# A RWKV-7 chunk scan with joint PSUM banks, and a Mamba-2 stage in another order: one encoder layer on one core

## The chip, the cores and the metric

The kernel runs as one program on one core of a Trainium2 chip. The metric is device time in microseconds, the median of several executions. For the kernel before, three executions gave 2464.68, 2473.31 and 2473.44 us, median 2473.31. Engine names are those of the profile: PE is TensorE's matmuls, PEld its weight loads, DVE VectorE, ACT ScalarE, POOL GpSimd, SP SyncE.

## The reference

One layer of a bidirectional encoder, 1024 tokens by 1024 channels, all in float32. One wide input projection feeds three branches (Mamba-2, RWKV-7, HGRN2) and three gates; each branch scans in both directions and adds the two; the branches are projected, gated and summed, projected again, and a SwiGLU feed-forward follows. The two parts that matter here:

```python
# Mamba-2, one direction, chunks of 128 tokens, 16 heads x 64, 2 groups, state 128
a_cum = cumsum(dt * a)                      # per head, within the chunk
y_diag = (C B^T * exp(a_cum[q] - a_cum[s]), s <= q) @ (x * dt)
chunk_state = B^T @ (x * dt * exp(a_cum[-1] - a_cum))
S = exp(a_cum[-1]) * S + chunk_state        # from chunk to chunk
y_off = (C @ S_prev) * exp(a_cum)
y = y_forward + y_backward + x * d_skip;  y = rmsnorm(y * silu(z))
# RWKV-7, per head 64 x 64 state, both directions
S_t = S_{t-1} diag(w_t) + (S_{t-1} (-kk_t)) (kk_t a_t)^T + v_t k_t^T;  y_t = S_t r_t
```

## The kernel before, in words

**Fillers.** The input projection is float32 in three passes: each step is three matmuls of 128x128 weights by 128x512 (lines 329 to 331, `mm<-x,wh` and `mm<-x,wl`), 16 steps to a job, into one of three PSUM banks of the tag `mm`. A job loads a weight tile `wr`, ScalarE casts it to `wh` (line 220), and VectorE or GpSimd makes the rest `wl` (line 222). The steps are dealt out between the work of the branches, so that PE has something to do in their waits: `J.fill(n)` issues n steps, `J.share(w)` issues the part `w / J.weight` of what is left. The tables `FILL` hold these numbers. The order on each engine is set by a scheduler, except where a block is under `manual_schedule`: there the named engine keeps the order in which the code is written. Finished halves are copied by ScalarE to `st` (line 271) and stored.

**RWKV chunk scan** (stage `r2`, lines 734 to 890, 444 to 637 us of the span). 16 chunks of 64 tokens, two directions d, 8 heads as 4 pairs. For each chunk and direction: `G`, products of B/K with A/R, 8 matmuls into two banks of the tag `g` (two banks in all, shared with the transposes `Bps`), masked into SBUF by VectorE in four operations (lines 805 and 807); `R` = G x SV, copied by ScalarE; `U` = T x R, which VectorE and ScalarE write negated into `UV`; `S` += B^T x UV, scaled by VectorE into the next chunk's `SV`; `Y` = UV x G + SV x A/R in two groups of 8. G of the next chunk is made while R, U and S of this one wait. Each direction has banks and tiles of its own, so most evacuations are 128x256. One filler step follows U, one follows Y. The scheduler orders PE.

**Mamba-2 stage** (`ssd`, 1128 to 1481 us). For each of two groups of 8 heads: convolutions (lines 1279 to 1289) of B, C and four tiles of x; C B^T (`CB`) and transposes of B and x to token-major `Bt`, `xt`; then a loop of 8 steps i, in which direction 0 handles chunk i and direction 1 chunk 7 - i. `pairs(c)` makes the 128 x 8 x 128 matrix E of chunk c: two DMAs fetch rows of `cumd` broadcast to all partitions, GpSimd subtracts the column values (line 1357), VectorE merges the two directions with a predicated copy (line 1360), ScalarE takes the exponential (1361), VectorE multiplies by CB (1362). It is called two steps ahead, rows and all. In each step and direction: `yo` = C x S, one matmul 128x512 (1378), `yt` = yo x e^cum on VectorE (1380), Y += yt on GpSimd (1381), `xw` = xt x weights on VectorE (1384), `st` = B x xw on PE (1386), S x decay on GpSimd (1390), S += st on VectorE (1391). Then 8 `yd` products with E as weights (128 columns) and 64 columns of xt moving (1397), added to Y by VectorE (1399). The skip term starts Y: GpSimd writes Y = xt x gd (1371). GpSimd's order in the loop is as written. After a group's loop, the end phase: silu of z (1408), 32 transposes of Y (1417), the product with z (1418), the store to `ysc`, squares (1425) and their sums (1426). Tiles `E`, the convolutions' and z's share five buffers (`EB = 5`).

Of the kernel before, what the change touches and what calls it, by code (L numbers as in the profile page):

```python
# [18 lines left out]
P = 128  # L19
# [19 lines left out]
    "ss": (4, 36, 12, 18, 6, 3, 8, 5, 22, 13, 8),  # L39
# [344 lines left out]
def rwkv(g):  # L384
# [349 lines left out]
    with ExitStack() as es:  # L734
# [16 lines left out]
        S = []  # L751
        for d in range(2):
            t = rp.tile([P, 4, 64], F32, tag=f"S{d}", name=f"S{d}", bufs=1)
            nc.gpsimd.memset(t, 0.0)
            S.append(t)
        NS = 16

        def load_early(c, d):
            if c >= NS:
                return None  # L760
            AR = rp.tile([P, 4, 2, 64], F32, tag=f"AR{d}", name="ARc", bufs=3)
            BK = rp.tile([P, 4, 2, 64], F32, tag=f"BK{d}", name="BKc", bufs=3)
            TT = rp.tile([P, 4, 64], F32, tag=f"TT{d}", name="TTc", bufs=3)
            nc.sync.dma_start(BK, BKs[d][:, c].rearrange("p q (s t) -> p q s t", s=2))
            nc.sync.dma_start(AR, ARs[d][:, c].rearrange("p q (s t) -> p q s t", s=2))
            nc.sync.dma_start(TT, TTs[:, d, c])
            return AR, BK, TT

        def loads(c, d, early):
            AR, BK, TT = early  # L770
            UV = rp.tile([P, 2, 4, 64], F32, tag=f"UV{d}", name="UVc")
            SV = rp.tile([P, 2, 4, 64], F32, tag=f"SV{d}", name="SVc")
            G = rp.tile([P, 2, 4, 2, 64], F32, tag=f"G{d}", name="Gc")
            cc = c if d == 0 else NS - 1 - c
            vs = Vs[cc // 2, (cc % 2) * 64:(cc % 2) * 64 + 64]
            for e in range(2):
                er = slice(e * 64, e * 64 + 64)
                nc.gpsimd.tensor_scalar(G[er, e, :, 0, :], AR[er, :, 0, :], 1.0, None, MUL)
            for t in (SV, UV):
                nc.sync.dma_start(t[64:128, 0], vs[:, 0])  # L780
                nc.sync.dma_start(t[0:64, 1], vs[:, 1])
            if c == 0:
                nc.gpsimd.memset(SV[0:64, 0], 0.0)
                nc.gpsimd.memset(SV[64:128, 1], 0.0)
            return AR, BK, UV, SV, TT, G

        def prep_b(c, d, ld):
            BK = ld[1]
            Bt = rp.tile([P, 4, P], F32, tag=f"Bt{d}", name="Btc")
            ps = pp.tile([P, 4, P], F32, tag="g", name="Bps", bufs=2)  # L790
            for p in range(4):
                nc.tensor.transpose(ps[:, p], BK[:, p].rearrange("p s t -> p (s t)"), g.ident)
            nc.scalar.copy(Bt, ps)
            return Bt

        def prep_g(c, d, ld):
            AR, BK, UV, SV, TT, G = ld
            pss = [pp.tile([P, 4, 2, 64], F32, tag="g", name="Gps", bufs=2) for e in range(2)]
            for p in range(4):
                for e in range(2):  # L800
                    er = slice(e * 64, e * 64 + 64)
                    nc.tensor.matmul(pss[e][:, p], BK[er, p], AR[er, p], start=True, stop=True)  # L802
# [7 lines left out]
        HD = [(h % 2, h // 2, slice(h % 2 * 64, h % 2 * 64 + 64)) for h in range(8)]  # L810

        def c_R(c, d, ld):
            AR, BK, UV, SV, TT, G = ld
            R = rp.tile([P, 4, 64], F32, tag=f"R{d}", name="Rc")
            psR = pp.tile([P, 4, 64], F32, tag="c", name="Rps", bufs=2)
            for e, p, er in HD:
                nc.tensor.matmul(psR[er, p], G[:, e, p, 0, :], SV[:, e, p, :], start=True, stop=True)
            nc.scalar.copy(R, psR)
            return R

        def c_U(c, d, ld, R):
            AR, BK, UV, SV, TT, G = ld
            psU = pp.tile([P, 4, 64], F32, tag="c", name="Ups", bufs=2)
            for e, p, er in HD:
                nc.tensor.matmul(psU[er, p], TT[er, p], R[er, p], start=True, stop=True)
            nc.vector.tensor_scalar(UV[0:64, 0], psU[0:64], -1.0, None, MUL)
            nc.scalar.mul(UV[64:128, 1], psU[64:128], -1.0)

        def c_S(c, d, ld, Bt, nxt):
            AR, BK, UV, SV, TT, G = ld  # L830
            psS = pp.tile([P, 4, 64], F32, tag="c", name="Sps", bufs=2)
            for e, p, er in HD:
                nc.tensor.matmul(psS[er, p], Bt[:, p, er], UV[:, e, p, :], start=True, stop=True)
            pc = PC[:, d, c].unsqueeze(2).broadcast_to([P, 4, 64])
            nc.vector.tensor_add(S[d], S[d], psS)
            SVn = nxt[3]
            nc.vector.tensor_mul(SVn[0:64, 0], S[d][0:64], pc[0:64])
            nc.vector.tensor_mul(SVn[64:128, 1], S[d][64:128], pc[64:128])
            nc.gpsimd.tensor_mul(S[d], S[d], pc)

        def c_Y(c, d, ld):
            AR, BK, UV, SV, TT, G = ld
            pool, tag, n = (pp, "y", 1) if d == 0 else (g.mmps, "mm", 3)
# [1280 lines left out]
```

## Time and profile before

| | us |
|---|---|
| median of 3 executions | 2473.31 |
| the profiled execution | 2473.65 |
| its span, first to last instruction | 2471.9 |
| outside the span | 1.75 |
| PE busy in the span | 2309.0 (93%) |
| granted TensorE clock, mean | 0.968 |
| RWKV chunk scan, 444 to 637 | 193 |
| Mamba-2 stage, 1128 to 1481 | 353 |

A page of the profile gives busy times by engine; views of the trace give groups of instructions by line, waits, and a timeline. A matmul's length in the timeline overlaps the next one's, so its cost is read from start to start. "Idle before" names what an engine waited for last. A float32 matmul shows as two records.

### The profile page before, as it was taken

The numbers are of one execution on the slowest core, as the hardware profiler recorded it, in microseconds if no ns is written. First come the engines' busy times: TensorE is split into PE (matmuls) and PEld (weight loads), VectorE is DVE, ScalarE is ACT, GpSimd is POOL, SyncE is SP. The second block draws the span as 40 slices with busy tenths as digits, with TensorE's granted clock in tenths as the row PEclk, the third lists the DMA queues.
The fourth block names the chain that finished last, engine by engine and source line by source line (L and its number), as shares of the span: only waits on it lengthen the run. The fifth ranks groups of instructions, "written<-read, shape, count | busy, mean of one in ns | idle before, by whom it ended". The sixth has DMA issues, their size and how long they took to land.

```text
span 2471.9 us, 37794 instructions
## 1 busy us (share of the span) xinstructions
PE 2309.0 (93%) x14785; PEld 1865.5 (75%) x14785; DVE 1633.4 (66%) x2130; ACT 989.0 (40%) x1460; POOL 1070.9 (43%) x863
## 2 busy tenths in 40 slices
PE   8998999999989889999899899999999999999985
PEld 6777778888867777778668667788788888877664
DVE  5678863456567867746666676643675455569999
ACT  6554532222454654436224236322433333344333
POOL 4433422444134543320661671421464444447885
PEclk9999999899999999999899999999899999999998
DMA  5456685654342232225635647632132222253311
GB/s 148 122 140 137 161 211 123 201 169 147 118 148 90 82 111 78 73 73 172 149 114 170 149 111 248 211 111 95 60 95 85 86 79 84 86 179 111 97 66 68
DMA packets 381215, 306.27 MB, mean 124 GB/s; under 512 B 111273, under 2 KB 323149, under 8 KB 381037
## 3 DMA queue, kind: packets, MB, share of 16 engines
q1 hardware_dynamic: 260909, 225.71, 30.8%
q10 hardware_dynamic: 119936, 77.61, 10.8%
q8 instruction: 117, 1.92, 0.3%
q0 software_dynamic: 192, 0.52, 0.1%
q14 instruction: 61, 0.50, 0.1%
HBM read 209.68 MB, written 94.11 MB: 123 GB/s over the span
## 4 chain that ended last, share of the span: by engine, by line
PE 60%; DVE 23%; POOL 5%; issue 5%; DMA 4%; ACT 3%; ACTq 0%; SPq 0%; DVEq 0%; POOLq 0%
PE mm L329 6%; PE mm L330 6%; PE mm L331 6%; PE ps L1576 6%; PE ps L1577 6%; PE ps L1578 6%; DVE acc L1915 3%; DVE ab L1793 2%; PE Gps L802 2%; PE mm L232 2%; PE mm L230 2%; PE mm L231 2%; DMA E<-cumd 2%; POOL E L1357 2%; DVE rb L1793 1%
## 5 line engine op out<-in xcount | busy, mean ns | idle before, releaser
L329 PE MATMUL mm<-x,wh 128*128 128x512 f32 (+1 forms) x1232 | 499.4, 405 | 0.5 <-ACT wh L220 0.5
L330 PE MATMUL mm<-x,wh 128*128 128x512 f32 (+1 forms) x1232 | 495.7, 402 | 0.0
L331 PE MATMUL mm<-x,wl 128*128 128x512 f32 (+1 forms) x1232 | 494.2, 401 | 0.2
L329 PEld LDWEIGHTS mm<-x,wh 128*128 128x128 f32 (+1 forms) x1232 | 234.1, 190 | 61.7 <-issue 10.6
L331 PEld LDWEIGHTS mm<-x,wl 128*128 128x128 f32 (+1 forms) x1232 | 233.9, 190 | 56.4 <-issue 6.0
L330 PEld LDWEIGHTS mm<-x,wh 128*128 128x128 f32 (+1 forms) x1232 | 234.4, 190 | 55.6 <-issue 6.8
L1578 PE MATMUL ps<-xb,rb 128*128 128x512 f32 x432 | 168.1, 389 | 0.0
L1576 PE MATMUL ps<-xb,rb 128*128 128x512 f32 x432 | 168.0, 389 | 0.0
L1577 PE MATMUL ps<-xb,rb 128*128 128x512 f32 x432 | 168.0, 389 | 0.0
L220 ACT CAST wh<-wr 128x1024 fp32r<-128x1024 f32 (+2 forms) x103 | 100.2, 973 | 118.8 <-PE mm L330 96.7
L1576 PE MATMUL ps<-rb,ab 128*128 128x512 f32 x308 | 125.8, 408 | 20.1 <-DVE acc L1915 19.1
L222 POOL TENSOR_TENSOR wl<-wr,wh 128x1024 fp32r<-128x1024 f32 x30 | 78.2, 2607 | 146.6 <-ACT wh L220 137.4
L222 DVE TENSOR_TENSOR wl<-wr,wh 128x1024 fp32r<-128x1024 f32 (+2 forms) x73 | 97.2, 1332 | 62.2 <-ACT wh L220 62.2
L1577 PE MATMUL ps<-rb,ab 128*128 128x512 f32 x308 | 122.4, 397 | 2.4 <-POOL rb L1793 2.4
L1578 PE MATMUL ps<-rb,ab 128*128 128x512 f32 x308 | 121.5, 397 | 1.5 <-DVE ab L1793 1.5
L1740 ACT CAST rb<-fs 128x512 fp32r<-128x512 f32 x85 | 52.5, 622 | 167.3 <-PE ps L1578 115.7
L271 ACT COPY st<-mm 128x512 f32<-128x512 f32 x130 | 75.6, 581 | 97.5 <-PE mm L331 77.8
L805 DVE TENSOR_TENSOR Gc<-Gps,mk 128x256 f32<-128x256 f32 x64 | 27.0, 422 | 112.0 <-PE Gps L802 59.1
L1915 DVE TENSOR_TENSOR acc<-acc,ps 128x512 f32<-128x512 f32 x148 | 94.1, 675 | 0.2 <-PE ps L1578 0.2
L1576 PEld LDWEIGHTS ps<-xb,rb 128*128 128x128 f32 x432 | 81.1, 188 | 16.9
L1578 PEld LDWEIGHTS ps<-xb,rb 128*128 128x128 f32 x432 | 81.1, 188 | 16.8
L1577 PEld LDWEIGHTS ps<-xb,rb 128*128 128x128 f32 x432 | 81.1, 188 | 16.7
(504 smaller groups left out, 5548.9 us busy)
## 6 DMA issues: line engine op xcount, KB each, us to landing
wr<-in_w_in_dram ACTq DMA_DIRECT2D x74, 512.0 KB
fr<-in_ffn_w_in_dram SPq DMA_DIRECT2D x44, 512.0 KB
E<-cumd SPq DMA_DIRECT2D x32, 512.0 KB
pg<-st ACTq DMA_DIRECT2D x48, 256.0 KB
gt<-pg SPq DMA_DIRECT2D x24, 512.0 KB
ad<-a SPq DMA_DIRECT2D x22, 512.0 KB
dr<-in_ffn_w_down_dram SPq DMA_DIRECT2D x22, 512.0 KB
ar<-ad SPq DMA_DIRECT2D x22, 512.0 KB
```

What stands on the lines that cost most here:

```text
L220: nc.scalar.copy(hi[:, :kt, :n], raw[:, :kt, :n])
L222: g.lo_eng.tensor_sub(lo[:, :kt, :n], raw[:, :kt, :n], f32(hi[:, :kt, :n]))
L271: g.nc.scalar.copy(st[:n], ps)
L329: g.nc.tensor.matmul(ps[:n], w[0][:, k, :n], xh, start=(k == 0), stop=False)
L330: g.nc.tensor.matmul(ps[:n], w[0][:, k, :n], xl, start=False, stop=False)
L331: g.nc.tensor.matmul(ps[:n], w[1][:, k, :n], xh, start=False, stop=(k == KT - 1))
L1576: nc.tensor.matmul(ps, ah, bh, start=(i == 0), stop=False)
L1577: nc.tensor.matmul(ps, ah, bl, start=False, stop=False)
L1578: nc.tensor.matmul(ps, al, bh, start=False, stop=(i == n - 1))
L1740: nc.scalar.copy(blk[:, 0], src[j])
L1793: eng.tensor_sub(blk[:, 1], s, f32(blk[:, 0]))
L1915: nc.vector.tensor_add(m[j], m[j], ps)
```

## The change

Two stages are rewritten; the rest keeps its text and gets new line numbers.

Chunk scan: both directions share tiles (`S`, `SV`, `UV`, `R`) and one PSUM bank for each of R, U, S and Y, so one evacuation of 128x512 stands for two of 128x256. Direction 1's G products go to the `mm` banks. The code of a chunk stands under `manual_schedule(engines={PE})`, so PE keeps the order as written: R, G of direction 0, U, filler, G of direction 1, S, B, Y, filler.

Mamba-2: the output is made channel-major. `yd` takes 64 columns of xt as weights and E (128 columns) as the moving side; `yo` takes four 128-column slices of the state as weights and C as the moving side; the transposes of the end phase disappear. e^cum is now the tile `X`, exponentials of the fetched rows on ScalarE, multiplied by yo on VectorE. Adding the column values is ScalarE's for direction 0 (eight 128x128 operations with a bias) and GpSimd's for direction 1. Direction 1's seven states are made in a prepass into `Sb`, between `pairs(0)` and `pairs(1)`; the loop carries only direction 0's state `Sa`, whose decay product is VectorE's. The skip term is put on E's diagonal by a second predicated copy (`id8`). silu(z) is made before the prepass and staged in DRAM (`zd`); each step loads its part, multiplies, stores to `ysc`, and adds the squares in small GpSimd operations. `rows(i + 2)` is called at the top of step i, `pairs(i + 2)` at its end. The table `FILL["ss"]` changes: 551 parts before, 573 after; between the first chunk's rows and the loop's end stand 187 of them for each group (7 x 5 + 8 x 10 + 8 x 9).

```diff
-    "ss": (4, 36, 12, 18, 6, 3, 8, 5, 22, 13, 8),
+    "ss": (4, 30, 12, 5, 10, 9, 22, 8, 5),
...
-        def prep_g(c, d, ld):
-            AR, BK, UV, SV, TT, G = ld
-            pss = [pp.tile([P, 4, 2, 64], F32, tag="g", name="Gps", bufs=2) for e in range(2)]
+        def prep_g(d, ld):
+            G = ld.G[d]
+            pool, tag, n = (pp, "g", 2) if d == 0 else (g.mmps, "mm", 3)
+            pss = [pool.tile([P, 512], F32, tag=tag, name="Gps", bufs=n).rearrange("p (q s t) -> p q s t", q=4, s=2)
+                   for e in range(2)]
...
+        def c_R(ld):
+            R = rp.tile([P, 2, 4, 64], F32, tag="R", name="Rc")
+            psR = bank("c", "Rps", 2)
+            for d, e, p, er in HD:
+                nc.tensor.matmul(psR[er, d, p], ld.G[d][:, e, p, 0, :], ld.SV[:, d, e, p, :], start=True, stop=True)
+            nc.scalar.copy(R, psR)
+            return R
...
+        order = ExitStack()
+        order.enter_context(tc.manual_schedule(engines={PE}))
         for c in range(NS):
...
+            R = c_R(ld)
             J.fill(F[0] + (F[6] if c < 2 else 0))
             if c + 1 < NS:
-                prep_g(c + 1, 0, nx[0])
-            for d in range(2):
-                c_U(c, d, ld[d], R[d])
+                prep_g(0, nx)
+            c_U(ld, R)
             J.fill(F[1])
             if c + 1 < NS:
-                prep_g(c + 1, 1, nx[1])
-                for d in range(2):
-                    c_S(c, d, ld[d], bt[d], nx[d])
+                prep_g(1, nx)
+                c_S(c, ld, bt, nx)
                 J.fill(F[2])
-                bt = [prep_b(c + 1, d, nx[d]) for d in range(2)]
-            for d in range(2):
-                c_Y(c, d, ld[d])
+                bt = [prep_b(d, nx) for d in range(2)]
+            c_Y(c, ld)
             J.fill(F[3])
...
+                for q in range(grp * 4, grp * 4 + 4):
+                    zs = sp.tile([P, L + 4], F32, tag="E", name="zs", bufs=EB)[:, :L]
+                    nc.sync.dma_start(zs, J.get(g.pz, q))
+                    nc.scalar.activation(zs, zs, AF.Silu)
+                    nc.sync.dma_start(zd[q], zs)
...
+                def pairs(c, Es):
+                    Xs = []
+                    for d in range(2):
+                        e, h0 = Es[d], d * 16 + grp * 8
+                        X = yp.tile([P, 4, P], F32, tag=f"X{d}", name="X", bufs=2)
+                        if c != (0, NT - 1)[d]:
+                            for b in range(2):
+                                hr = slice(b * 64, b * 64 + 64)
+                                nc.scalar.activation(X[hr], e[hr, b::2], AF.Exp)
+                        if d == 0:
+                            for h in range(8):
+                                nc.scalar.activation(e[:, h], e[:, h], AF.Identity, bias=cums[:, c, h0 + h:h0 + h + 1])
+                        else:
+                            nc.gpsimd.tensor_tensor(e, e, cums[:, c, h0:h0 + 8].unsqueeze(2).broadcast_to([P, 8, P]),
+                                                    ADD)
...
                     nc.vector.tensor_mul(e, e, CB[:, c:c + 1, :].broadcast_to([P, 8, P]))
+                    nc.vector.copy_predicated(e, id8.unsqueeze(1).broadcast_to([P, 8, P]),
+                                              gd[:, c].unsqueeze(2).broadcast_to([P, 8, P]))
...
+                def state(d, c, old, new):
+                    xw = yp.tile([P, 512], F32, tag="xw", name="xw", bufs=2)
+                    nc.vector.tensor_tensor(h3(xw), h3(xt[:, c]), per_head(wst, c, d), MUL)
+                    ps = pp.tile([P, 512], F32, tag="b", name="st", bufs=2)
+                    nc.tensor.matmul(ps, Bt[:, c], xw, start=True, stop=True)
+                    if old is None:
+                        nc.vector.tensor_copy(new, ps)
+                    else:
+                        (nc.vector if d == 0 else nc.gpsimd).tensor_tensor(h3(new), h3(old), per_head(dec, c, d), MUL)
+                        nc.vector.tensor_add(new, new, ps)
...
+                nxt = [pairs(0, rows(0))]
+                ahead = rows(1)
+                for c in range(NT - 1, 0, -1):
+                    state(1, c, Sb[:, c] if c < NT - 1 else None, Sb[:, c - 1])
+                    J.share(F[3])
+                nxt.append(pairs(1, ahead))
                 for i in range(NT):
...
+                    e, X = nxt.pop(0)
+                    if i + 2 < NT:
+                        ahead = rows(i + 2)
+                    part = []
+                    for d, S in ((1, Sb[:, i] if i < NT - 1 else None), (0, Sa if i else None)):
...
+                        for q in range(4):
+                            nc.tensor.matmul(ps[:, q], S[:, q * P:(q + 1) * P], CT[:, ts], start=True, stop=True)
+                        nc.vector.tensor_mul(X[d], X[d], ps)
+                        part.append(X[d])
+                    if i < NT - 1:
+                        state(0, i, Sa if i else None, Sa)
+                    J.share(F[4])
...
+                        nc.tensor.matmul(ps[h % 2 * 64:h % 2 * 64 + 64, h // 2], xt[:, i, h * 64:h * 64 + 64], e[:, h],
                                          start=True, stop=True)
...
+                        nc.gpsimd.tensor_add(y, y, part[1])
+                    nc.vector.tensor_add(y, y, ps)
+                    nc.vector.tensor_mul(z, z, y)
+                    nc.sync.dma_start(ysc[grp * 4:grp * 4 + 4, :, ts].rearrange("q p t -> p q t"), z)
+                    nc.scalar.activation(y, z, AF.Square)
...
+                    if i + 2 < NT:
+                        nxt.append(pairs(i + 2, ahead))
                     J.share(F[5])
```

How the order on the engines moves. PE in one chunk of the scan, before (R, G, U, S, B and Y are the `ps` tiles; each row is one line's matmuls in succession):

```order
L817 MATMUL Rps<-SVc,Gc 64x64 x16
L802 MATMUL Gps<-ARc,BKc 128x128 x8
L825 MATMUL Ups<-Rc,TTc 64x64 x16
L802 MATMUL Gps<-ARc,BKc 128x128 x8
L848 MATMUL Yps<-Gc,UVc 64x64 x2
L833 MATMUL Sps<-UVc,Btc 64x64 x16
L792 MATMUL Bps<-ident,BKc 128x128 x4
L848 MATMUL Yps<-Gc,UVc 64x64 x4
L792 MATMUL Bps<-ident,BKc 128x128 x4
L848 MATMUL Yps<-Gc,UVc 64x64 x3
L850 MATMUL Yps<-ARc,SVc 64x64 x8
```

And in the changed kernel, where `mm` are filler matmuls:

```order
L823 MATMUL Rps<-SV,Gc 64x64 x16
L806 MATMUL Gps<-ARc,BKc 128x128 x8
L830 MATMUL Ups<-Rc,TTc 64x64 x16
L329 MATMUL mm<-x_208,wh 128x512
L330 MATMUL mm<-x_209,wh 128x512
L331 MATMUL mm<-x_208,wl 128x512
L806 MATMUL Gps<-ARc,BKc 128x128 x8
L837 MATMUL Sps<-UV,Btc 64x64 x16
L793 MATMUL Bps<-ident,BKc 128x128 x8
L849 MATMUL Yps<-Gc,UV 64x64 x16
L852 MATMUL Yps<-ARc,SV 64x64 x16
```

The second G group now has a filler step ahead of it, and S, B and Y stand in whole groups.

VectorE in the Mamba-2 loop, before (`m` is the mask of the predicated copy, the two `S` the two directions' states):

```order
L1360 COPY_PREDICATED E<-m_10446,E 128x1024
L1384 TENSOR_TENSOR xw<-xt,wst 128x512
L1391 TENSOR_TENSOR S_10889<-S_10889,st 128x512
L1362 TENSOR_TENSOR E<-E,CB 128x1024
L1380 TENSOR_TENSOR yt<-yo,ecum 128x512
L1399 TENSOR_TENSOR Y<-Y,yd 128x512
L1391 TENSOR_TENSOR S_10888<-S_10888,st 128x512
```

And after, about one step of the loop:

```order
L1380 COPY_PREDICATED E<-m_10222,E 128x1024
L1436 TENSOR_TENSOR X<-X,yd 128x512
L1424 TENSOR_TENSOR X<-X,yo 128x512
L1399 TENSOR_TENSOR Sa<-Sa,dec 128x512
L1437 TENSOR_TENSOR z<-z,X 128x512
L1393 TENSOR_TENSOR xw<-xt,wst 128x512
L1400 TENSOR_TENSOR Sa<-Sa,st 128x512
L1382 TENSOR_TENSOR E<-E,CB 128x1024
L1383 COPY_PREDICATED E<-id_10223,gd 128x1024
```

The decay, the z product and the id8 copy are new on VectorE; the predicated copy of a later chunk stands ahead of the addition of `yd`.

GpSimd in the same loop, before:

```order
L1390 TENSOR_TENSOR S_10888<-S_10888,dec 128x512
L1357 TENSOR_TENSOR E<-E,cums 128x1024 x2
L1381 TENSOR_TENSOR Y<-Y,yt 128x512
L1390 TENSOR_TENSOR S_10889<-S_10889,dec 128x512
L1381 TENSOR_TENSOR Y<-Y,yt 128x512
```

And after:

```order
L1376 TENSOR_TENSOR E<-E,cums 128x1024
L1435 TENSOR_TENSOR X<-X 128x512
L1442 TENSOR_TENSOR X<-X 128x256
L1444 TENSOR_TENSOR ss<-X 128x128
```

One E product instead of two, one addition instead of two, no state products in the loop, and the two small sums.

More of the change, by code (lines that the diff above doesn't have):

```diff
@@ L808, in prep_g @@
                                         mk[d][e][kr, 0].unsqueeze(1).broadcast_to([64, 4, 64]), MUL)
[L810 to L817, printed above, removed]
+        HD = [(d, h % 2, h // 2, slice(h % 2 * 64, h % 2 * 64 + 64)) for d in range(2) for h in range(8)]
@@ L1343, in h3, with rows @@
                     return t.rearrange("p (h v) -> p h v", v=64)
-                S = [yp.tile([P, 512], F32, tag=f"S{d}", name=f"S{d}") for d in range(2)]
-                J.share(F[3])
-                def pairs(c):
+                def rows(c):
                     Es = []
```

248 lines of the change are left out of this document (105 added, 143 removed).

## The prediction

> **What bounds the kernel now.** The page first: TensorE (PE) is busy for 93% of the span, so time can only be won where PE's work shrinks or where it waits. Then the two stages that the change touches, by windows (length; busy us of PE, PEld, DVE, ACT, POOL; granted clock, DMA share, GB/s):
>
> ```profile
> PE 2309.0 (93%) x14785; PEld 1865.5 (75%) x14785; DVE 1633.4 (66%) x2130; ACT 989.0 (40%) x1460; POOL 1070.9 (43%) x863
> ```
>
> ```profile
> 444.00:637.00 193.00, 191.65 (x3240) 163.07 (x3239) 110.99 (x266) 50.91 (x116) 74.29 (x92) 0.96 0.52 159
> ```
>
> ```profile
> 1128.00:1186.00 58.00, 58.00 (x310) 48.12 (x309) 37.74 (x39) 36.42 (x50) 2.52 (x8) 1.00 0.50 133
> 1186.00:1300.00 114.00, 100.70 (x414) 71.89 (x414) 77.64 (x70) 26.36 (x30) 80.69 (x49) 0.91 0.49 130
> 1300.00:1375.00 75.00, 75.00 (x377) 63.27 (x376) 47.87 (x44) 35.82 (x45) 11.39 (x17) 1.00 0.56 170
> 1375.00:1481.00 106.00, 96.03 (x411) 68.88 (x409) 75.92 (x70) 27.06 (x32) 79.32 (x49) 0.95 0.54 128
> ```
>
> 444 to 637 is the RWKV chunk scan, where PE seems never to wait. The other four rows are the Mamba-2 stage, 353 us: convolutions of group 0, its chunk loop, convolutions of group 1, its loop. The convolution parts, 58 + 75 = 133 us, are full of PE work. In the loops, 114 and 106 us, PE is idle for 13 and 10 us and runs at clocks of 0.91 and 0.95, and POOL has more to do than DVE.
>
> Whether the scan is full of work is seen in the timeline of one chunk (start, length, operation; then VectorE at the same time):
>
> ```profile
> 466.31 1.15 PE L817 MATMUL Rps<-SVc,Gc 128*64 128x64 f32 x32
> ...
> 582.23 1.15 PE L817 MATMUL Rps<-SVc,Gc 128*64 128x64 f32 x32
> 583.31 1.16 PE L802 MATMUL Gps<-ARc,BKc 64*128 64x128 f32 x16
> 584.40 1.15 PE L825 MATMUL Ups<-Rc,TTc 64*64 64x64 f32 x32
> 585.48 1.94 PE L802 MATMUL Gps<-ARc,BKc 64*128 64x128 f32 x16
> 587.35 0.45 PE L848 MATMUL Yps<-Gc,UVc 128*64 128x64 f32 x4
> ...
> 593.86 1.15 PE L817 MATMUL Rps<-SVc,Gc 128*64 128x64 f32 x32
> ...
> 619.77 1.15 PE L817 MATMUL Rps<-SVc,Gc 128*64 128x64 f32 x32
> ```
>
> ```profile
> 584.51 0.42 DVE L805 TENSOR_TENSOR Gc<-Gps,mk 128x256 f32<-128x256 f32 x1 [1.74 <-PE Gps L802]
> ...
> 585.75 0.41 DVE L807 TENSOR_TENSOR Gc<-Gps,mk 64x256 f32<-64x256 f32 x1
> ```
>
> Both G groups are the same work, but from start to start the first takes 584.40 - 583.31 = 1.09 us, the second 587.35 - 585.48 = 1.87: it waits for the two banks that VectorE empties until 586.16. So 0.78 us of each chunk is a wait that is counted as busy. A chunk takes (619.77 - 466.31) / 13 = 11.80 us, the one shown 593.86 - 582.23 = 11.63.
>
> **Chunk scan: -13 us.** PE keeps the same matmuls. The second G group now takes its banks from the fillers' three, so its wait goes: 11.63 - 0.78 = 10.85; I take 10.8, 1.0 less in each of those 13 chunks. The joint evacuations (128x512 for two of 128x256) lie beside PE and count nothing. What covers each operand in the new order: the copy of R lies under the first G group (1.09), UV (after four evacuations of 0.42) under the fillers and the second G group, the next SV under B, Y and the fillers. With 0.78 in each chunk and no more it is -10; if new waits eat it, zero (a rival); PE gets no new work, so a loss could only come from those waits.
>
> **Mamba-2: PE's work.** The filler line by total and in the two loops, PE's pace on fillers, and three prices (start to start):
>
> ```profile
> L330 PE MATMUL mm<-x,wh 128*128 128x512 f32 x314 | 129.7, 413 | 0.0
> ```
>
> ```profile
> 1186.00:1300.00 114.00, 33.78 (x76) 14.87 (x76) 0.91 0.49 130
> 1375.00:1481.00 106.00, 31.61 (x76) 14.11 (x75) 0.95 0.54 128
> ```
>
> ```profile
> 1233.11 0.40 PE L329 MATMUL mm<-x,wh 128*128 128x512 f32 x1
> ...
> 1236.06 0.39 PE L330 MATMUL mm<-x,wh 128*128 128x512 f32 x1
> ...
> 1236.96 1.12 PE L1386 MATMUL st<-xw,Bt 128*128 128x512 f32 x2 [0.29 <-DVE S L1391]
> 1237.53 0.79 PE L329 MATMUL mm<-x,wh 128*128 128x512 f32 x1
> 1238.15 0.39 PE L330 MATMUL mm<-x,wh 128*128 128x512 f32 x1
> ...
> 1239.98 1.45 PE L1397 MATMUL yd<-xt,E 128*128 128x64 f32 x12
> 1241.23 0.47 PE L329 MATMUL mm<-x,wh 128*128 128x512 f32 x1
> ```
>
> ```profile
> 1155.88 1.06 PE L1312 MATMUL cbps<-CT,BT 128*128 128x128 f32 x8
> 1156.69 0.48 PE L329 MATMUL mm<-x,wh 128*128 128x512 f32 x1
> ```
>
> From 1233.11 to 1236.06 lie 13 filler matmuls: 0.227 us each, 0.68 per step of three. A state product `st` with one filler behind it takes 1.19, so 0.96 by itself; `yo` has the same shape. A `yd` record takes 1.25 / 12 = 0.104, 16 to a chunk. A 128x128 float32 product takes 0.81 / 4 = 0.20.
>
> A loop has 76 steps (51.8) + 28 `st` and `yo` (26.9) + 8 chunks of `yd` (13.3) = 92 us of PE work now. After, the shares put 7x5 + 8x10 + 8x9 = 187 of 573 parts of the same 314 steps between the first chunk's rows and the loop's end: 102 steps (69.5), 14 `st` (13.4), 14 `yo` of four 128x128 products (11.2), and `yd` with 64 columns as weights. That form isn't in the stage; nearest is R, 16 products of 64 columns on half the output rows in 1.08 us. `yd` has 8 with 128 columns: 1.08 a chunk (bounds 0.54 and today's 1.66), 8.6. Sum **103**.
>
> The 2 x 26 steps that move into the loops leave the convolution parts: 133 - 52 x 0.68 = 97.6. The 32 transposes of group 0's end phase go too (about 0.1 each), 3: **94**. Group 1's 32 lie behind 1481, in projections full of PE: -2.
>
> **Mamba-2: VectorE and POOL.** Means by line over the stage, then minimum/median/maximum of three groups, and POOL's two:
>
> ```profile
> L1384 DVE TENSOR_TENSOR xw<-xt,wst 128x512 f32<-128x512 f32 x28 | 39.9, 1427 | 0.6 <-ACT xt L1335 0.6
> L1360 DVE COPY_PREDICATED E<-m,E 128x1024 f32<-128x1024 uint8 x16 | 35.0, 2185 | 34.0 <-POOL E L1357 34.0
> L222 DVE TENSOR_TENSOR wl<-wr,wh 128x1024 fp32r<-128x1024 f32 x19 | 27.7, 1459 | 21.6 <-ACT wh L220 21.6
> L1362 DVE TENSOR_TENSOR E<-E,CB 128x1024 f32<-128x1024 f32 x16 | 24.0, 1502 | 2.8 <-ACT E L1361 2.8
> ```
>
> ```profile
> L1384 DVE TENSOR_TENSOR xw<-xt,wst x28: 674/1519/2382, 1181.9 to 1466.7; 128x512 f32<-128x512 f32 x28
> ```
>
> ```profile
> L1360 DVE COPY_PREDICATED E<-m,E x16: 1319/2378/2392, 1187.7 to 1461.5; 128x1024 f32<-128x1024 uint8 x16
> ```
>
> ```profile
> L1380 DVE TENSOR_TENSOR yt<-yo,ecum x28: 677/678/692, 1208.6 to 1479.7; 128x512 f32<-128x512 f32 x28
> ```
>
> ```profile
> L1381 POOL TENSOR_TENSOR Y<-Y,yt x28: 1253/1273/2255, 1209.4 to 1480.5; 128x512 f32<-128x512 f32 x28
> ```
>
> ```profile
> 1255.09 1.90 POOL L1357 TENSOR_TENSOR E<-E,cums 128x1024 f32<-128x1024 f32 x1
> ```
>
> `xw`, both inputs in SBUF, takes 0.67 us alone and 2.38 at worst; `yt`, one input from PSUM, is always 0.68. So in these loops VectorE loses time beside POOL. After, a group has 16 predicated copies (the id8 ones new), 8 E products, 14 `xw`, 6 decays (from POOL), 8 z products, 36 operations on PSUM at 0.68, and 6.4 `wl`. At minima (E and `wl` at means): 21.1 + 12.0 + 28 x 0.67 + 24.5 + 9.3 = 86; at means: 35.0 + 12.0 + 28 x 1.43 + 24.5 + 9.3 = 121. POOL's work falls to 8 E adds (15.2), 7 y adds, 6 decays and 8 sets of small sums at no more than 1.25 each (26): at most 42 us, 36% of 118 instead of 80.69 / 114 = 71%. Half the contention: 86 + 35 / 2 = **103**.
>
> The Trainium skill (SBUF — State Buffer, "Who interferes with whom") says that a VectorE instruction with two SBUF inputs shares a read port with GpSimd as an exclusive lock, and one with a single SBUF input doesn't contend. The two rows above agree. It speaks against the change in so far as each new VectorE operation but the PSUM ones is of the kind that locks; taken at the row's means its sum is the 121 above, the second rival.
>
> ACT gets four 64x512 exponentials and eight small biased copies a chunk and is at 26.36 of 114 now; it stays behind both. The silu of z moves ahead of each prepass: 4 loads and 4 stores of 512 KB on SP's queue in front of the first rows, and 8 z loads and 8 stores of 256 KB in the loop instead of the end phase. 8 x 0.5 MB at the window's 133 GB/s is 32 us of transfers (estimate) beside parts where the DMA share is 0.50; counted at nothing, and if the first rows wait behind one of them, 4 us a group. Before, a loop took 114 and 106 us for 92 of PE work, 1.20 times it, with DVE and POOL at 76 to 81. After, PE and VectorE have 103 each; POOL's chain (E add, Y adds, state products in one queue) is gone and rows come two chunks early. I take 1.14 times: **118** a group (112 to 124). Stage: 94 + 2 x 118 = 330, -23, and -2.
>
> **Sum.** 2473.65 (span 2471.9 + 1.75) - 13 - 23 - 2 = **2435.7** us. The profiled run is 0.3 above the median, 2473.31, so nothing is added. With 112 a group, or with 124 and the scan at -10: 2424 to 2451.
>
> **Rivals.**
> 1. PE sets the pace: VectorE keeps up, 105 a group, stage 304, total 2473.65 - 13 - 49 - 2 = 2410. For it: PE's 103 and VectorE's 103 lie side by side. Against: in-order queues on both, and cold clocks at each loop's start.
> 2. VectorE sets the pace at before's means: 121 plus 10 of the 36 us that it idles in a loop now (114 - 77.64), 131 a group, stage 356: 2473.65 - 13 + 3 - 2 = 2462, on the border of no change. For it: the id8 copies and decays. Against: POOL half empty.
> 3. The scan's fixed order: SV, UV or a bank comes late by 1 us in each chunk, all behind it on PE waits, and the 13 are lost: 2449.
> 4. Slower: the loop from one chunk's z to the next. z product, ACT square, POOL's two sums, ACT's exponentials into the freed X tile, POOL's E add (the next y add queued behind it), then VectorE's predicated copy, which stands ahead of the next chunk's X additions in VectorE's queue. ACT's price by its nearest rows:
>
> ```profile
> L621 ACT ACTIVATE E<-sg x16: 615/632/654, 87.5 to 324.0; 128x512 f32<-128x512 f32 x16
> ```
>
> ```profile
> ACT st L271 <- PE mm L331: 12.6, 2, 7.6
> ```
>
> Chain: 0.6 + 2 x 1.25 + 2 x 0.63 + 1.9 = 6.3 at most, against seven VectorE operations ahead of the copy, 5.9 to 8.5: just covered. The round then is 6.3 + 2.4 + two X operations (1.4) + z (up to 1.4) = 11.5 us a chunk, below 118 / 8. It decides if ACT's queue adds waits: the row shows it stuck behind a filler bank twice for 12.6 us. At 5.5 a chunk the round is 17 us: 8 x 17 + 18 of state prepass = 154 a group, stage 402, total 2508. Against: such waits occurred twice in a loop, not eight times; slower than the bound below from 144 a group.
>
> **How the numbers follow.** Forecast 0.55, rival 1 0.10, rival 2 0.17, rival 3 0.08, rival 4 0.10. A measurement tells about 0.5%, 12.4 us: faster is below 2461, slower above 2486. Rival 2 is halved between faster and the same. Faster: 0.55 + 0.10 + 0.08 + 0.08 = 0.81; same 0.09; slower 0.10. The range 2408 to 2466 leaves out rival 4, the lower half of 1 and the upper part of 2. The forecast's own is 2424 to 2451.
>
> **What would show it.** Right: R to R in 10.8 us, both G groups 1.09; the loops with their prepass some 118 us, POOL below 42% there, medians of `xw` and copies well below 1.52 and 2.38, clock above 0.95. Wrong: a chunk period of 11.8, a group above 137 (94 + 2 x 137 = 368 eats the scan's gain), ACT squares or X exponentials waiting in each chunk, `yd` above 1.66 a chunk.

## The result and the profile after

| | before | after |
|---|---|---|
| median, us | 2473.28 | 2504.78 |
| executions | 2464.68 to 2473.44 | 2499.74 to 2509.68 |
| profiled execution; span | 2473.65; 2471.9 | 2509.68; 2508.0 |
| first R to last Y of the scan | 189.1 | 176.2 |
| Mamba-2, first transposes of dt to first branch projection | 352.4 | 391.2 |

Slower: the ratio is 1.0129 (95% interval 1.0112 to 1.0145), 2504.78 - 2473.28 = 31.5 us more where 38 less were forecast, and outside the range. Between its first R and its last Y the scan gave what was forecast; the Mamba-2 stage lost 39. (Between the two stages some of the scan's gain is lost again: the stage starts only 6.4 us earlier, at 1122.7 instead of 1129.1.)

The page's line on the engines, to compare with that of before: PE has less to do (2287.0 for 2309.0 us) in a longer span.

```profile
PE 2287.0 (91%) x14889; PEld 1848.3 (74%) x14889; DVE 1623.9 (65%) x2101; ACT 1055.9 (42%) x1620; POOL 986.1 (39%) x817
```

One chunk of the new scan on PE:

```profile
581.87 1.15 PE L823 MATMUL Rps<-SV,Gc 128*64 128x64 f32 x32
582.95 1.16 PE L806 MATMUL Gps<-ARc,BKc 64*128 64x128 f32 x16
584.04 1.15 PE L830 MATMUL Ups<-Rc,TTc 64*64 64x64 f32 x32
...
586.02 1.16 PE L806 MATMUL Gps<-ARc,BKc 64*128 64x128 f32 x16
587.12 1.15 PE L837 MATMUL Sps<-UV,Btc 128*64 128x64 f32 x32
...
589.22 1.15 PE L849 MATMUL Yps<-Gc,UV 128*64 128x64 f32 x32
...
591.38 0.50 PE L329 MATMUL mm<-x,wh 128*128 128x512 f32 x1
...
592.27 1.15 PE L823 MATMUL Rps<-SV,Gc 128*64 128x64 f32 x32
```

Both G groups last 1.09 to 1.10 us from start to start; the wait of 0.78 is gone, and R to R is 592.27 - 581.87 = 10.40. That is 1.23 less than the chunk of before that the prediction shows. Y is the other part: its two groups take 591.38 - 589.22 = 2.16 us. Before, the same products stood in five pieces, 0.38 us at 587.35 and four pieces from here to the next R at 593.86, 2.44:

```profile
591.42 0.68 PE L848 MATMUL Yps<-Gc,UVc 128*64 128x64 f32 x14
```

So Y in whole groups saves 0.66 us, and the fillers take 0.2 more.

The Mamba-2 stage by windows, cut at the first and last z product of each group (columns as before), and the filler line L330 in the last two:

```profile
1122.70:1180.00 57.30, 57.30 (x307) 47.74 (x307) 37.61 (x39) 38.88 (x53) 0.39 (x6) 1.00 0.53 165
1180.00:1231.00 51.00, 44.40 (x189) 32.04 (x187) 23.64 (x27) 21.32 (x43) 11.56 (x8) 0.93 0.66 167
1231.00:1294.00 63.00, 59.27 (x335) 45.54 (x334) 52.96 (x56) 33.67 (x68) 27.50 (x22) 1.00 0.57 144
1294.00:1337.00 43.00, 29.14 (x156) 23.89 (x155) 27.16 (x26) 20.27 (x29) 9.32 (x10) 0.84 0.44 136
1337.00:1375.00 38.00, 37.92 (x187) 31.49 (x186) 22.65 (x23) 24.03 (x34) 1.85 (x8) 1.00 0.63 202
1375.00:1423.00 48.00, 43.60 (x181) 31.20 (x180) 24.94 (x30) 22.08 (x45) 11.56 (x8) 0.96 0.76 182
1423.00:1513.00 90.00, 47.01 (x248) 34.27 (x246) 57.13 (x62) 44.82 (x84) 34.80 (x33) 0.64 0.43 121
```

```profile
1375.00:1423.00 48.00, 18.55 (x47) 8.64 (x46) 0.96 0.76 182
1423.00:1513.00 90.00, 2.45 (x7) 1.13 (x6) 0.64 0.43 121
```

No engine is full in the last 90 us: PE 47, DVE 57, ACT 45, POOL 35. PE has 7 filler steps there, idles half the time, and its clock drops to 0.64. Over the stage PE idles 390.3 - 318.6 = 72 us, against 353 - 329.7 = 23 before; its work is 11 us less. 51 and 48 us pass at the start of a group before the first z. Group 1 from its last transposes to its outputs, first after, then before:

```profile
1373.14 1.03 PE L1335 MATMUL xps<-ident,xq 128*128 128x128 f32 x8
```

```profile
1422.56 0.69 DVE L1437 TENSOR_TENSOR z<-z,X 128x512 f32<-128x512 f32 x1
1433.62 0.68 DVE L1437 TENSOR_TENSOR z<-z,X 128x512 f32<-128x512 f32 x1
1458.85 0.69 DVE L1437 TENSOR_TENSOR z<-z,X 128x512 f32<-128x512 f32 x1
...
1513.45 0.69 DVE L1437 TENSOR_TENSOR z<-z,X 128x512 f32<-128x512 f32 x1
```

```profile
1373.87 1.03 PE L1334 MATMUL xps<-ident,xq 128*128 128x128 f32 x8
```

```profile
1397.99 0.67 DVE L1399 TENSOR_TENSOR Y<-Y,yd 128x512 f32<-128x512 f32 x1
...
1477.70 0.69 DVE L1399 TENSOR_TENSOR Y<-Y,yd 128x512 f32<-128x512 f32 x1 [1.39 <-POOL Y L1381]
```

From the transposes to the first output: 49 us after, 24 before. From there to the last: 91 after, 80 before. The round is 10 to 15 us (6 at the last), with one hole of 25. Group 0 reads alike: last transposes at 1174.73, first z at 1231.16, last at 1336.26, one step of 27 us in between. That is 56 us to the first output where 27 passed before, and 105 for the loop where 84 did.

The two groups don't cost alike, though. From the first transposes of dt to group 1's last transposes pass 250.4 us after and 244.8 before: group 0's longer chain costs only 6 us in the end, as group 1's convolutions and fillers run beside it, fillers that group 1 then lacks. Group 1 has no such work beside it; from its last transposes to its last output pass 140.3 us where 103.8 did, and these 36 are most of the stage's loss.

The hole in group 1, in ScalarE's queue, where `gt` are the gates of the next stage:

```profile
1436.40 0.61 ACT L1440 ACTIVATE X<-z 128x512 f32<-128x512 f32 x1
1447.34 1.28 ACT L1498 ACT_TABLE_LOAD   x1 [10.32 <-issue]
1448.63 1.06 ACT L1498 ACTIVATE gt<-gt 128x1024 f32<-128x1024 f32 x1
1449.69 1.28 ACT L1371 ACT_TABLE_LOAD   x1
1450.98 1.27 ACT L1371 ACTIVATE X<-E 64x512 f32<-64x512 f32 x2
```

A sigmoid of the next stage stands ahead of the exponentials for the next chunk, waits 10 us for its data, and everything behind it waits too. Its load, on SyncE's queue, waited for the store of what it reads, `pg`; the queue's wait (total, times, longest) and the load:

```profile
SPq L1497 <- DMA pg<-st: 9.0, 1, 9.0
```

```profile
1443.83 1.27 SPq L1497 DMA_DIRECT2D gt<-pg  x2
```

So SyncE's queue was held up as well. The hole in group 0 is of the same kind: a convolution of group 1 waits for its load.

```profile
1307.72 1.24 ACT L1286 ACTIVATE acc<-pt,vcolsv 128x1024 f32<-128x1024 f32 x1 [9.97 <-DMA pt<-px]
```

And the start of group 0, on SyncE's queue, then on GpSimd:

```profile
1175.80 0.37 SPq L1357 DMA_DIRECT2D E<-cumd  x1
1176.26 2.56 SPq L1342 DMA_DIRECT2D zd<-zs  x2
1178.91 0.75 SPq L1357 DMA_DIRECT2D E<-cumd  x1
1179.76 6.05 SPq L1342 DMA_DIRECT2D zd<-zs  x1
1187.65 2.94 SPq L1357 DMA_DIRECT2D E<-cumd  x2
```

```profile
1197.61 1.89 POOL L1376 TENSOR_TENSOR E<-E,cums 128x1024 f32<-128x1024 f32 x1 [39.41 <-ACT X L1371]
...
1218.98 1.43 POOL L1399 TENSOR_TENSOR Sb<-Sb,dec 128x512 f32<-128x512 f32 x1 [3.03 <-DVE Sb L1400]
1220.37 2.34 POOL L1376 TENSOR_TENSOR E<-E,cums 128x1024 f32<-128x1024 f32 x1
```

The rows of E stand between the stores of silu(z), in whose buffers they land; the first E addition starts at 1197.6, 23 us after the last transposes (20 in group 1: 1392.9 for 1373.1). Then come the six decays of the prepass, each waiting for a state from VectorE, and only at 1220.4 the addition for chunk 1.

### The profile page after: what moved, and what is told of

Read it like the earlier page. It is cut to its first block, busy times and chain, and to the rows that moved or that the text cites. A ratio compares the mean times of both kernels' runs of the same rounds, so it can differ in the third digit from the quotient of the medians.

```text
span 2508.0 us, 37981 instructions
## 1 busy us (share of the span) xinstructions
PE 2287.0 (91%) x14889; PEld 1848.3 (74%) x14889; DVE 1623.9 (65%) x2101; ACT 1055.9 (42%) x1620; POOL 986.1 (39%) x817
## 3 DMA queue, kind: packets, MB, share of 16 engines
q1 hardware_dynamic: 277805, 234.10, 31.5%
## 5 line engine op out<-in xcount | busy, mean ns | idle before, releaser
L330 PE MATMUL mm<-x,wh 128*128 128x512 f32 (+1 forms) x1232 | 494.5, 401 | 0.0
L330 PEld LDWEIGHTS mm<-x,wh 128*128 128x128 f32 (+1 forms) x1232 | 235.4, 191 | 52.5 <-issue 4.5
L230 PE MATMUL mm<-oh,wh 128*128 128x512 f32 x224 | 89.2, 401 | 8.4 <-DVE gt L1507 4.2
L1605 PEld LDWEIGHTS ps<-xb,rb 128*128 128x128 f32 x432 | 81.1, 188 | 17.0
L1604 PEld LDWEIGHTS ps<-xb,rb 128*128 128x128 f32 x432 | 81.1, 188 | 16.8
```

Source lines behind the costliest of these rows:

```text
L230: nc.tensor.matmul(ps, whi[:, k, :n], xh, start=(k == 0), stop=False)
L330: g.nc.tensor.matmul(ps[:n], w[0][:, k, :n], xl, start=False, stop=False)
L1604: nc.tensor.matmul(ps, ah, bl, start=False, stop=False)
L1605: nc.tensor.matmul(ps, al, bh, start=False, stop=(i == n - 1))
```

## The experiments

Each run is set against runs of the kernel before on the same chip (2471.8 to 2474.1); against the changed kernel means against 2504.78, the median of four executions from 2499.74 to 2509.68, so that differences of a few us to it say little.

**Which stage.** The new scan alone, then the new Mamba-2 stage alone (each in the text of the kernel before, with its `FILL` line).

> The kernel before with the new chunk scan alone (its Mamba-2 stage is the old one). Theory: the scan gains about 13 us between its first R and its last Y (189.1 before, 176.2 in the changed kernel's trace), and some 6 of them are given back in the HGRN stage behind it; the time is 2461 to 2468 us. Rival: the Mamba-2 stage of the changed kernel is slow because it starts on other clocks and queues behind the new scan; then this kernel carries part of the loss and is 2473 or more.

> The kernel before with the new Mamba-2 stage alone. Theory: the whole loss is here, 35 to 39 us, so 2508 to 2513. Rival (the scan's order hurts what follows): under 2495.

2461.72 (ratio 0.9967, 0.9953 to 0.9981) and 2507.82 (1.0149, 1.0129 to 1.0168). As expected: the scan alone gains 10, the Mamba-2 stage alone loses 36. With the scan alone the last Y ends the scan 177.6 us after its first R, 11.5 less than before, and 18.8 us earlier in the span, but the Mamba-2 stage starts only 8.8 us earlier (1120.3 for 1129.1). What takes back the rest between them was not tested.

**Is it the scheduler's order?** The scheduler moved most fillers ahead of group 1's loop. Theory A: ScalarE's order, or PE's, as written.

```diff
-                order.enter_context(tc.manual_schedule(engines={POOL}))
+                order.enter_context(tc.manual_schedule(engines={POOL, ACT}))
```

> The changed kernel with ScalarE's order in the Mamba-2 loop as written, beside GpSimd's. Theory A (next-stage work and fillers hoisted by the scheduler): ScalarE's gate sigmoids no longer stand ahead of the X exponentials, and with them PE's fillers stay in the loop (46 to 50 matmuls a chunk in the last loop instead of 45, 13, 0, 0, 0, 0), so group 1's prepass and loop fall from 138 us to 115 to 120 and the total to 2470 to 2482. Theory B (VectorE and the chain from one z to the next set the period): 138 stays above 130, total 2495 or more.

> The changed kernel with PE's order in the Mamba-2 loop as written, beside GpSimd's; ScalarE's order stays the scheduler's. Theory A: fillers stay in the loop (48 a chunk), the clock stays full, total 2475 to 2490; what the hoisted gate sigmoids cost is still there, about 10. Theory B: 2495 or more. If a written order makes PE wait for each late operand, it is slower than the changed kernel, 2515 or more.

2615.9 and 2529.93: both far slower than the changed kernel, so theory A falls in this form. The narrower one, PE as written in group 1's loop only:

```diff
                 for i in range(NT):
+                    if grp == 1 and i == 0:
+                        order.enter_context(tc.manual_schedule(engines={PE}))
```

> The changed kernel with PE's order as written in group 1's loop only, so that 48 filler matmuls stay in each of its chunks (the scheduler left 45, 13, 0, 0, 0, 0 in the last six) and are missing where they had been moved to. Theory E (the fillers run out, PE stands idle at half clock in the last loop): the last loop is paced by PE at 14 to 15 us a chunk, what lies ahead of it is shorter, total 2475 to 2492. Rival (fillers only move the hole to another place): 2500 or more.

2518.14. Its windows are the end of group 0's loop to the end of group 1's convolutions, the start of group 1, and group 1's loop:

```profile
1323.00:1362.70 39.70, 12.01 (x60) 10.34 (x58) 24.99 (x26) 16.12 (x21) 1.46 (x8) 0.59 0.28 84
1362.70:1411.10 48.40, 22.87 (x51) 10.58 (x49) 22.28 (x26) 21.76 (x43) 11.72 (x8) 0.60 0.63 146
1411.10:1514.80 103.70, 103.70 (x579) 83.62 (x580) 65.49 (x68) 48.21 (x94) 32.63 (x33) 1.00 0.54 148
```

The loop is now full, with 112 filler steps (L330) and a clock of 1.00. But the first stretch has none left, and PE idles 28 us there and 26 in the start. The hole has moved and grown. So the empty last loop is a symptom: the stage's chains are longer than the fillers last, wherever these stand. Theory E falls.

**The chain from z to z.** The squares go to B's tile, dead in the loop, instead of the X tile, and `pairs(i + 2)` is called ahead of them:

```diff
+                    if i + 2 < NT:
+                        nxt.append(pairs(i + 2, ahead))
+                    if i < 6:
+                        y = BT[:, hs(i % 2)].rearrange("p (q t) -> p q t", t=P)
                     nc.scalar.activation(y, z, AF.Square)
...
-                    if i + 2 < NT:
-                        nxt.append(pairs(i + 2, ahead))
```

> The changed kernel with the squares of z written to a tile that is free (B's, dead in the loop) instead of the X tile, and the E matrix of chunk i + 2 called ahead of the squares: the chain from one chunk's z over square, sums, exponentials and E product to the next z is cut. Theory C with this chain as the round (rival 4 of the prediction): the last chunks of group 1, 11 to 13 us apart from z to z, come down to 9 to 10.5, total 2488 to 2496. Rival: another wait, VectorE's queue, sets the round, and the spacing and the time stay within 4 us.

2487.29, 17.5 less than the changed kernel. The chain was there. The time is 0.7 under the range, but the spacing in group 1 stays at 11.3 to 14.5 us outside the hole (21.2 here), and only the last two steps shrink, to 7.6 and 1.3. So the round has more in it than the squares. Which of the edit's two parts did it was not separated.

**The gates in ScalarE's queue.** Four copies of one element tie the first gates to the last sum.

```diff
             gt = g.r32.tile([P, L], F32, tag="r0", name="gt", bufs=4)
+            if b == 1 and f < 4:
+                nc.vector.tensor_copy(gt[0:1, 0:1], ss[0:1, L - 1:L])
```

> The changed kernel with the first four gate tiles of the next stage made to wait for the last sums (one more VectorE element copy each), so that their sigmoids can't stand in ScalarE's queue inside group 1's loop. Theory: the hole of 10.3 us before a gate sigmoid and its activation tables (1.28 us, six times) go, total 2488 to 2496. Rival: another wait takes the place, within 4 us of the changed kernel.

> Gates held back and squares apart. If the two waits are separate, the gains of 17 (squares apart) and 8 to 16 (gates) add up: 2470 to 2482. If they are one wait, 2486.

2495.32, 9.5 less; no step of group 1 is longer than 15.2 us there, while group 0 keeps its hole of 25.6. The edit takes the gates out of ScalarE's and of SyncE's queue, so it doesn't say which of the two held the chunk up. Both edits together give 2478.11 (1.0026, 1.0011 to 1.0040), 26.7 less: the two add up (17.5 + 9.5 = 27.0). The first and last z of group 1 then stand at 1414.86 and 1485.44: 70.6 us for the loop, less than the 79.7 of before. With PE as written on top:

> Gates held back, squares apart, and PE's order as written in group 1's loop. Theory E: 2455 to 2470, at or under the kernel before. Rival: the written order costs more than the fillers bring, 2480 or more.

2513.53, 35 more than without: the written order costs again.

**The start of a group.** z staged ahead of the convolutions; the prepass written ahead of the first E products; both with the squares apart; one state instead of seven (six are left out, and the loop reads the one for every chunk); the decays on VectorE. The edits, in this order, cut:

```diff
+                for q in range(grp * 4, grp * 4 + 4):
+                    zs = sp.tile([P, L + 4], F32, tag="E", name="zs", bufs=EB)[:, :L]
...
                 conv(8 + grp, BT)
...
-                nxt = [pairs(0, rows(0))]
-                ahead = rows(1)
+                first, ahead = rows(0), rows(1)
...
-                nxt.append(pairs(1, ahead))
+                nxt = [pairs(0, first), pairs(1, ahead)]
...
-                    state(1, c, Sb[:, c] if c < NT - 1 else None, Sb[:, c - 1])
+                    if c == 1:
+                        state(1, c, None, Sb[:, 0])
...
-                    for d, S in ((1, Sb[:, i] if i < NT - 1 else None), (0, Sa if i else None)):
+                    for d, S in ((1, Sb[:, 0] if i < NT - 1 else None), (0, Sa if i else None)):
...
-                        (nc.vector if d == 0 else nc.gpsimd).tensor_tensor(h3(new), h3(old), per_head(dec, c, d), MUL)
+                        nc.vector.tensor_tensor(h3(new), h3(old), per_head(dec, c, d), MUL)
```

> The changed kernel with the silu of z and its four stores put ahead of a group's convolutions, so that they no longer share buffers and SyncE's queue with the first rows of E. Theory C (the chain ahead of and around the loop is longer than PE's fillers last, so PE stands idle in group 1's loop; what shortens the chain shortens the time): the first E product comes 10 to 15 us earlier in each group, total 2475 to 2488. Theory D (the order of instructions by the scheduler alone makes the loss): the time stays at 2500 to 2510.

2492.98: 11.8 less, 5 above the range. And not as expected: the first E additions start 6 and 7 us earlier, but the first z of the groups does not (1235.9 and 1423.5, for 1231.2 and 1422.6). The gain is in the loops. The gates' sigmoids stand at 1406 to 1417 here, ahead of group 1's loop, so its hole is gone, and the loop takes 78 us instead of 91: this gain overlaps with the one of the late gates.

> The changed kernel with the prepass written ahead of the first E products: GpSimd's six decays no longer stand behind an E product that waits for its rows (39 to 41 us). Theory C: the prepass runs while the rows come, z of chunk 0 comes some 10 us earlier in each group, total 2482 to 2492. Rival: the rows are late anyway and the E products now stand behind the decays, 2500 or more.

2501.79: 3 less, within the spread; the rival's answer.

> The three edits together. Theory C: gains add up, 2440 to 2465, below the kernel before if the sum is over 32. Theory D: 2500 or more.

2493.94: the gains do not add up; 32 were to be had if they did, and the squares alone gave 17.5. Group 1's last transposes come 7 us later here than in the changed kernel (1380.4 for 1373.1), and 53 us pass from them to the first z, where 49 do in the run with the squares alone.

> The changed kernel with one state product of direction 1 in the prepass instead of seven (six are left out, all chunks read the one that is made). Theory F (two chains in a row: the serial prepass is added ahead of a loop whose round stays at some 12 us, so each group is longer by it): six links of 2.3 us, 14 a group less, total 2475 to 2485. Rival G (the start waits for rows and GpSimd's queue, the prepass lies under that): 2496 or more.

> The changed kernel with the prepass decays on VectorE too, so that a link of the prepass has no change of engine: 1.4 us instead of 2.3. Theory F: 6 a group less, total 2488 to 2497. Rival G: GpSimd's E product of chunk 1 comes sooner since no decay stands ahead of it, which gives the same or more; the two are told apart by the run with one state. If neither holds, 2500 or more.

2490.62 and 2491.27: 14 and 13.5 less. The first is half of what theory F named and lies between the two answers (the start falls from 56 and 49 us to 46 and 40); the second is F's, but shows no more than that the links matter.

> Squares apart, gates held back, z staged ahead of the convolutions, prepass decays on VectorE: all that was found, in one correct kernel. The gains measured alone are 17, 10, 12, and some 10 for the decays by theory F; half of the last two is taken as already counted: 2460 to 2472. The kernel with the new scan alone, 2462, stays the mark.

2480.92 (1.0033, 1.0020 to 1.0047): 8.9 above the range, no better than squares and gates alone. Either two pieces of the start hide each other, or the start is not the rest. The last two runs have squares apart, gates late and one state (six states are left out), and the second also z early.

> Squares apart and gates held back (2478 together), and one state product of direction 1 in the prepass instead of seven (six are left out). Theory F (what is left over is the time from a group's last transposes to its first z, 50 us against 24 before): the 14 of the one-state run come on top, 2460 to 2467. Rival (the gains only cover each other, as in the kernel of all that was found, 2481): 2473 or more.

> The same and z staged ahead of the convolutions, 12 by itself. Theory F: 2450 to 2458, under the kernel with the new scan alone (2462). Rival: no faster than the kernel without the move of z, within 4 us of it.

2482.71 and 2456.34 (0.9928, 0.9915 to 0.9942). The first is the rival's answer, the second is in theory F's range. Group 1's last transposes and first E addition, in the first run and then in the second, and the first and last z of the second:

```profile
1367.08 1.04 PE L1335 MATMUL xps<-ident,xq 128*128 128x128 f32 x8
```

```profile
1387.57 1.90 POOL L1376 TENSOR_TENSOR E<-E,cums 128x1024 f32<-128x1024 f32 x1 [45.45 <-DMA E<-cumd]
```

```profile
1363.14 1.03 PE L1340 MATMUL xps<-ident,xq 128*128 128x128 f32 x8
```

```profile
1364.26 1.90 POOL L1375 TENSOR_TENSOR E<-E,cums 128x1024 f32<-128x1024 f32 x1 [27.43 <-ACT X L1370]
```

```profile
1389.00 0.69 DVE L1437 TENSOR_TENSOR z<-z,X 128x512 f32<-128x512 f32 x1
...
1461.02 0.69 DVE L1437 TENSOR_TENSOR z<-z,X 128x512 f32<-128x512 f32 x1
```

Without the six states the rows are still late behind the z stores: 20 us after the transposes, as in the changed kernel. With the z stores ahead of the convolutions it is 1 us, and 26 go at once. The first z then comes 26 us after the transposes (24 to the first output before), and the loop takes 72.

Four kernels with squares apart and gates late make a table: 2478.11 with nothing more; 2482.71 with one state; 2480.92 with z early (and the decays on VectorE); 2456.34 with one state and z early. From the transposes to the first z of group 1 they take 50, 40, 43 and 26 us. So the start has two chains side by side, the rows behind the z stores and the serial prepass, and either alone holds it at 40 to 43 us. Two things stay open. With one state alone the start gets 10 us shorter, but the loop 9 us longer (80 for 71), and why is not shown. And the one-state kernels also leave out twelve `st` products, some 12 us of PE's work at 0.96 each, so not all of the 24.6 us between the last two is the chain's.

**VectorE's load.** The masked copy of the diagonal is left out, and with it the skip term.

```diff
-                    nc.vector.copy_predicated(e, id8.unsqueeze(1).broadcast_to([P, 8, P]),
-                                              gd[:, c].unsqueeze(2).broadcast_to([P, 8, P]))
```

> The changed kernel without the second predicated copy, so without the skip term (part of the computation left out): 16 VectorE operations of 1.3 to 1.8 us go. If VectorE's load sets the round (rival 2 of the prediction), 1.3 or more a chunk goes, 20 in all, 2485 or less. If the chain sets it, the copy lies beside it: within 6 of the changed kernel.

2494.72, 10 less: between the two answers, inconclusive. The copy takes 1.31 us at the median, and the chain that ended last passes through it in the last chunk of the changed kernel (at 1508.9).

## Why the prediction was wrong

- **Chunk scan, -13.** Right in mechanism: the second G group takes 1.09, and PE waits 0.7 us in all from 455 to 610, so the covers held and rival 3 did not come. The size, 189.1 to 176.2 us from first R to last Y, is in part luck. A chunk takes 10.40 where 10.8 was forecast, because Y in whole groups was not counted; over the 14 steps from the second R to the last, R to R falls from 11.69 to 10.48, 17 us, and the first chunk is 4.5 shorter. Against that the last chunk is 8.6 us longer, since 16 filler steps stand in it, for 2 before. By itself the scan is worth 10 of the whole time.
- **PE's work in Mamba-2.** Right where it can be read: `yd` takes 1.0 us a chunk (1.08), four `yo` products 0.81 to 0.91 (0.80) with a filler behind them. PE's busy time fell by 22 us in all. But the same 314 filler steps were assumed, and 297 are in the stage: the scan took 20 more than before. And 102 steps were put between the first rows and the end of each group's loop. In group 0 there are 129; in group 1 there are 47 in the start and 7 in the loop. The order of the changed kernel's instructions shows that, and it was not counted.
- **VectorE and POOL.** Right in direction: `xw` fell from 1.52 to 0.68 us at the median, POOL is busy 31% and 34% of the groups' starts and loops, the id8 copy takes 1.31. The masked copy stayed at 2.34, which was not forecast. In group 1's loop neither engine is full.
- **"I take 1.14 times: 118 a group."** This step failed. The windows of a group with its prepass (1180 to 1337 and 1375 to 1513) take 157 and 138 us, while the convolutions take 95 as forecast (94). The step took the larger of two engine loads and a factor from the old loops. In a stage in which no engine is full, the time is a chain's: last transposes to last z took 162 and 140 us; to the last output before, 111 and 104. The round of a chunk was found rightly, 11.5 in rival 4 (10 to 15 measured), but without the hole it is hardly shorter than the old loop's, 79.7 / 7 = 11.4, and the prepass is put in front of it. That start has no term of its own in the forecast: it is 56 and 49 us, where 27 and 24 sufficed before. Rival 4 gives it 18 us; no row shows that figure, and leaving out six of the seven states shortened the start by 10. The rows behind the z transfers were "counted at nothing", or 4 us a group: moving the stores brought the first E addition from 20 us behind the transposes to 1.
- **Rival 4** gave 2508, near the 2504.78, in part by luck. Its chain was there and ScalarE's queue did add waits; the runs price the squares at 17.5 and the gates at 9.5. But not as it said: no 5.5 us in each chunk, but one long hole in each group, from later work that the scheduler had put into the queue; and the start is about three times its 18 us.
- **Rivals 1 and 2** need a full PE or VectorE. Neither came.

Open: the parts of the loss are not independent. Of the 31.5 us, squares and gates account for 27 with the whole computation kept. The start, in the presence of these edits, is worth up to 22 more (2478.11 - 2456.34), with six states left out. Group 0's hole was not tested by itself. How a kernel that keeps all its states would shorten both chains of the start was not found: with z early and the decays on VectorE it stays at 2480.92. There group 0 ends 27 us earlier than in the changed kernel (1309.6 for 1336.3), but group 1's last transposes come only 5 earlier; PE is busy for 57.9 of the 58.2 us between. So earlier work in group 0 doesn't pass on to group 1 where PE is full. The best run with the whole computation is the one with the new scan alone, 2461.72, faster than both kernels.

## What to carry to other kernels

When a change moves work between engines in a stage in which none is full, follow the chain from one output to the next and from the stage's start to its first output, through every queue, and price that; engine loads are only a lower bound. A prepass is added to the rounds, as it was here, unless they get shorter or other work lies beside it: in group 0 most of it was covered, in the last group nothing was left to cover it. Count the fillers in the new order, and see what of the next stage the scheduler has put into the queues.

## What the hardware showed

- A `float32` matmul with 512 moving columns takes 0.96 us (by the rows that the prediction shows) and four with 128 take 0.81 to 0.91 with a filler behind them: dividing the moving side cost nothing here.
- From 1440 to 1452 PE was busy for 2.75 of 12 us. From 1452 to 1470 its granted clock was 0.50, against 1.00 from 1423 to 1440, and eight `yo` records took up to 2.08 us instead of 1.16. So the idle PE lengthened the very chain that it waited for. Two such groups of the changed kernel's last loop:

```profile
1433.15 1.16 PE L1423 MATMUL yo<-CT,Sa 128*128 128x128 f32 x8 [0.58 <-DVE Sa L1400]
...
1464.05 2.08 PE L1423 MATMUL yo<-CT,Sb 128*128 128x128 f32 x8 [0.78 <-DVE Sa L1400]
```
